# Reordering and pacing the dense work beside the first recurrence of a two-layer hybrid backbone

## Chip, cores and metric

One core of one Trainium2 chip runs the whole program. The metric is the device time of one execution in microseconds; the lower the better.

## What is computed

A backbone of two layers over a stream of 1024 latent tokens and 256 context tokens, width 1024. The context is a prefix that goes through the same weights and never reads the latents. Cut to what matters here:

```
for l in range(DEPTH):                        # DEPTH = 2
    last = l == DEPTH - 1
    ux = _modulate(h, norm1_g[l], sh1, sc1) @ w_in[l]          # latents
    uc = _modulate(hc, norm1_g[l], mc[0], mc[1]) @ (w_in[l])   # context
    # bidirectional RWKV-7: context scan from zero state, latent scan from the context's final state
    y_rwkv_x, y_rwkv_c = _rwkv_mixer(ux[..., :RWKV_COLS], uc[..., :RWKV_COLS], not last, ...)
    # four head groups of 256 channels: RWKV, pooling, Fourier, convolution; then one projection
    h = h + gt1 * _mix_and_project(ux, y_rwkv_x, *other)       # concat(...) @ w_out
    h = h + gt2 * _swiglu(_modulate(h, norm2_g[l], sh2, sc2), ffn_w_in[l], ffn_w_out[l])
    if not last:
        hc = hc + mc[2] * _mix_and_project(uc, y_rwkv_c, *other)
        hc = hc + mc[5] * _swiglu(_modulate(hc, norm2_g[l], mc[3], mc[4]), ffn_w_in[l], ffn_w_out[l])
return _rmsnorm(h, final_norm_g)
```

In the last layer the context is needed for the scan's starting state only: it has no output projection and no feed-forward there. `_swiglu` has a hidden width of 2816, that is 22 blocks of 128 ("features" below), each with a gate half and an up half.

## The kernel before

Channels lie on the 128 partitions, tokens along the free dimension. The latents are two blocks of 512 tokens (tb 0 and 1), the context one block of 256 (tb 2). A float32 product is made of three products of split operands: a high part (an ACT cast, line 318) and a low part (a subtraction on DVE or POOL, line 319), so that one block product over k channel blocks is 3k matmuls. All matmuls are issued from line 151, so the profile tells them apart by the PSUM tile: `ps`, `pb`, `pc` for the recurrence and the feed-forward, `pf` for the dense work beside the recurrence.

A layer runs in this order:

1. `rwkv1`: the first dense blocks, with the convolution beside them.
2. `rwkv2`: the recurrence, ten steps: two of the context (`it` 0 and 1), eight of the latents (`it` 2 to 9). Each step handles 128 tokens in each direction. Three iterations before step 0 only prepare. In a pass of the loop `chain` advances step `it`, `front_b` makes step `it + 1` ready, `inner` builds the triangular blocks of step `it + 2`, sends them through DRAM (lines 980 and 986, the tile `Ad`), solves them on DVE (lines 1026 to 1035) and sends the result through DRAM again (lines 1039 and 1045, `Td`), and `prep` makes the scaled inputs of step `it + 3` (up to line 956). `finish` reads out a block when both directions have passed it (the stores of line 1238). For the context this is at step 2, and sets `R.ctx`. A pass has 14 gaps (`GAPS`).
3. In each gap `W.fill(FILL[l][...])` lets a generator `fill()` issue dense work worth so many microseconds by its own count (256 columns x 6 matmuls count 0.64). The three numbers of `FILL[l]` hold for the first two passes, the third, and step 0 onwards. A yield of None ends a call without work. `fill()` goes through the rest of the input projection, the Fourier mixer (`four2`), the output projection of all groups but RWKV for the latents and of all groups for the context (`outp`), the context's second norm (`norm2c`) and its feed-forward for the first `NC` features (`ffn1_ctx`: four weight loads of 256 KB, split by ACT and POOL, 48 matmuls of 256 columns, a SiLU on line 1625). `side()` runs convolution and pooling and sets `R.sided` at its end.
4. Behind the recurrence: the RWKV part of the latents' output projection and their second norm (`ffn1_acts`), with what is left in `fill()` beside it.
5. `ffn1`: 22 features with the latents' products in a seven-product form, a copy `P1` on line 1564 each. For features from `NC` on, in layer 0, it also makes the context's products (48 matmuls of 256 columns) from weights that are split already, with one more split (`a21`).
6. The second half of the feed-forward and, in layer 0, the next layer's norm and first blocks.

Instructions are not issued in the program's order alone: a planner orders each engine's queue by the program's order and a simulated readiness, including whether a tile of a pool is free. The pool of general tiles, `t2`, has 73 (`T2`); the recurrence's rings (`rg`) take theirs once and give them back after their last use. Weight splits of `outp` use the pools `m2` and `f2`, those of `ffn1_ctx` `m2` and `c2`. All DMAs are issued from SP's queue in order. During the recurrence `lo_eng` is POOL.

Of the kernel before, what the change touches and what calls it, by code (L numbers as in the profile page):

```python
# [22 lines left out]
NFF = 22  # L23
# [18 lines left out]
MODPE = ((3, 0),)  # L42
MK = 7
FR = "c2"
FILL = ((2.6, 1.2, 0.9), (2.3, 1.0, 0.9))
LA = 2
NC = 14
ORD = (1, 0)
OFILL = (1.0, 0.3, 0.8, 1.0)
LOP = (0, 2, 4)  # L50
# [40 lines left out]
class _Kernel:  # L91
# [701 lines left out]
    def rwkv2(s, R, fill):  # L793
# [7 lines left out]
        for it in range(-3, N):  # L801
# [9 lines left out]
            for g in range(GAPS):  # L811
# [21 lines left out]
                W.step()  # L833
                W.fill(FILL[R.l][min(max(it + 2, 0), 2)])
            for _ in ch:
# [6 lines left out]
        while W.live:  # L842
            W.step()
            W.fill(FILL[R.l][2])

# [398 lines left out]
    def run(s, nlayers):  # L1244
# [43 lines left out]
        for l in range(nlayers):  # L1288
            last = l == L - 1
            segs = ("x",) if last else ("x", "c")  # L1290
            tbs = [tb for tb in range(3) if TBS[tb][0] in segs]
            swA, swB = [s.t2(), s.t2()], [s.t2(), s.t2()]
            ymix = [s.dr.tile([128, 1280], F32, name=s.nm("ymix")) for k in range(NK)]
            ho = [s.dr.tile([128, 1280], F32, name=s.nm("ho")) for k in range(NK)]
            hd = [s.dr.tile([128, 1280], F32, name=s.nm("hd")) for _ in range(NK)]
# [13 lines left out]
            R = _Rwkv()  # L1309
            R.conv1 = R.pool1 = R.rest2 = R.sided = R.ctx = False  # L1310

            def fill():
                for x in s.rest(l, R, acts, segs):
                    s.mod_step()
                    yield x
                assert not s.mods
                R.rest2 = True
                yield from s.four2(R, segs, swB, ymix)
                while not R.sided or not (last or R.ctx):
                    yield None  # L1320
                for tb in tbs[::-1]:
                    yield from s.outp(l, tb, hd, ho, ymix)
                if not last:
                    yield from norm2c()
                    for f in range(NC):
                        yield from s.ffn1_ctx(l, f, [a[2] for a in acts2], hid[f])

            def norm2c():

                for _ in range(2):  # L1330
                    yield
                s.lab("norm2")
                hc = s.rows(NK, ("c",))
                for k in range(NK):
                    h2[k][2] = hc[k][2]
                    nc.sync.dma_start(hc[k][2], ho[k][:, 1024:1280])
                yield
                r = yield from s.rstd_g([h2[k][2] for k in range(NK)], 256, D, 0, False, "ps", lambda j: s.t2())
                for k in range(NK):
                    acts2[k][2] = s.act_row(("c",))[2]  # L1340
                for _ in s.norm_g(l, 1, h2, 2, acts2, r):
                    if _ % 2:
                        yield
# [9 lines left out]
            s.weave.start(side())  # L1353
            s.rwkv1(l, R, first, acts, ("x", "c") if not last else ("x",), segs, swA, ymix, start)
            s.rwkv2(R, fill())
            h, acts = h2, acts2

# [131 lines left out]
    def ffn1_weights(s, l, ctx):  # L1489
# [11 lines left out]
        def sp(x):  # L1501
            hi, lo = s.t2(F32R, "f2"), s.t2(F32R, "f2")
            nc.scalar.copy(hi, x)  # L1503
            s.nw += 1
            (nc.gpsimd if s.nw % 7 in LOP else nc.vector).tensor_tensor(lo, x, hi.bitcast(F32), ALU.subtract)  # L1505
            return hi, lo
# [3 lines left out]
        for f in range(NFF):  # L1510
# [9 lines left out]
            yield sp(a12)  # L1520
            if ctx and f >= NC:
                yield sp(a21)
# [6 lines left out]
    def ffn1(s, l, wg, acts, B, bc, hid):  # L1529
# [4 lines left out]
        def take():  # L1534
            while len(q) <= LA:
                w = next(wg, None)
                if w is None:
                    break
                q.append(w)
            return q.pop(0)  # L1540
# [15 lines left out]
        for f in range(NFF):  # L1556
            s.lab("ffn")
            ctx = bc[0] is not None and f >= NC
            w = take()
# [316 lines left out]
```

## Time and profile before

| | |
|---|---|
| three runs, median (lowest to highest) | 3379.47 us (3378.45 to 3383.02) |
| profiled execution, its time | 3374.46 us |
| span from the first to the last instruction | 3372.7 us |
| mean granted TensorE clock | 0.907 |
| PE, DVE, ACT, POOL busy | 88%, 64%, 37%, 42% of the span |

Busy shares are means over stages that differ. `pf<-t,c` in a row means: the tile `pf` is written from tiles `t` and `c`, buffer numbers left out. A windows row gives the stretch in us from the span's start, its length, then for each engine the busy time in us and in brackets the number of instructions, then the granted clock, the busy share of the DMA engines and GB/s. PEld is the weight load, which overlaps PE. With a tile's name the row counts that tile's instructions alone, while clock and DMA stay those of the whole stretch. The stretches of the steps are cut at the first chain copy of each step (line 1139).

### The profile page before, as it was taken

To read this page: it belongs to the slowest core of one execution; us is meant where nothing else is said; L and a number is where in the kernel's file an instruction comes from. 1 tells how busy PE (TensorE), PEld (TensorE's weight loads), DVE (VectorE), ACT (ScalarE), POOL (GpSimd) and SP (SyncE) were. 2 spreads that over 40 slices of the span, in tenths; PEclk is the share of its full clock that TensorE was granted. 3 is DMA by queue.
4 is the path that set the end of the run, shared out by engine and by line. 5 is a ranking of instruction groups with operands and counts; after the bars stand their busy time and mean duration, and the time that the engine had idled before them with its cause. 6 is when DMAs were issued, how large, how long until landed. Compare 5 with 4: busy or idle time off the path is not lost.

```text
span 3372.7 us, 52579 instructions
## 1 busy us (share of the span) xinstructions
PE 2980.7 (88%) x18872; PEld 2405.8 (71%) x18872; DVE 2147.3 (64%) x3683; ACT 1260.6 (37%) x2575; POOL 1413.6 (42%) x1570
## 2 busy tenths in 40 slices
PE   6968897787998999999999978887877699999998
PEld 3757765665687788888888766655655478888887
DVE  6799756657556988644445598665666665555435
ACT  4455434443464222223212455343333433333312
POOL 2366324555258554435310064244542265444600
PEclk8979887787899999999999988977876899999999
DMA  7433335455464444337412212444553422223512
GB/s 263 152 99 103 100 114 139 132 154 156 135 228 131 145 137 153 118 98 232 142 35 77 87 53 94 119 139 124 162 151 76 139 76 75 91 79 124 179 39 77
DMA packets 375820, 415.50 MB, mean 123 GB/s; under 512 B 115587, under 2 KB 214916, under 8 KB 375558
## 3 DMA queue, kind: packets, MB, share of 16 engines
q1 hardware_dynamic: 375558, 412.13, 39.4%
q8 instruction: 149, 2.44, 0.3%
q14 instruction: 113, 0.93, 0.1%
HBM read 306.49 MB, written 100.27 MB: 121 GB/s over the span
## 4 chain that ended last, share of the span: by engine, by line
PE 58%; DVE 20%; DMA 12%; issue 4%; ACT 2%; POOL 2%; SPq 2%; DVEq 0%; POOLq 0%; ACTq 0%
PE pc L151 18%; PE ps L151 17%; PE pb L151 14%; PE pf L151 9%; DVE c L525 3%; DMA t<-Ad 3%; DMA Td<-t 2%; DVE t L1033 1%; DVE t L1026 1%; DVE t L941 1%; DMA t<-Td 1%; DVE t L255 1%; DMA t<-in_wmod 1%; DVE t L1035 1%; DVE g L1034 1%
## 5 line engine op out<-in xcount | busy, mean ns | idle before, releaser
L151 PE MATMUL pc<-t,f 128*128 128x512 f32 (+1 forms) x3108 | 750.2, 391 | 34.4 <-ACT t L420 21.4
L151 PEld LDWEIGHTS pc<-t,f 128*128 128x128 f32 x3108 | 580.2, 195 | 164.0 <-ACT t L420 25.3
L151 PE MATMUL ps<-t,f 128*128 128x512 f32 (+1 forms) x2094 | 519.9, 393 | 20.1 <-ACT t L318 7.9
L151 PE MATMUL pb<-t,f 128*128 128x512 f32 (+1 forms) x2094 | 468.5, 369 | 10.9 <-ACT t L1456 6.7
L151 PEld LDWEIGHTS ps<-t,f 128*128 128x128 f32 x2094 | 391.3, 190 | 101.5 <-ACT t L318 8.4
L151 PEld LDWEIGHTS pb<-t,f 128*128 128x128 f32 x2094 | 369.4, 189 | 81.4 <-ACT t L1456 7.4
L1503 ACT CAST f<-c 128x512 fp32r<-128x512 f32 x316 | 195.8, 621 | 531.0 <-PE ps L151 122.1
L1505 POOL TENSOR_TENSOR f<-c,f 128x512 fp32r<-128x512 f32 x135 | 184.3, 1365 | 428.2 <-ACT f L1503 404.3
L151 PE MATMUL pf<-t,f 128*128 128x512 f32 (+2 forms) x1500 | 311.2, 362 | 22.2 <-DMA f<-eo 8.3
L318 ACT CAST f<-m 128x512 fp32r<-128x512 f32 (+1 forms) x236 | 135.4, 576 | 437.3 <-PE pb L151 228.4
L151 PEld LDWEIGHTS pf<-t,f 128*128 128x128 f32 (+1 forms) x1500 | 247.6, 197 | 67.4 <-issue 9.7
L523 POOL TENSOR_TENSOR c<-c,cp 128x352 f32<-128x352 f32 (+2 forms) x168 | 186.3, 1109 | 152.1 <-ACT c L516 91.5
L1505 DVE TENSOR_TENSOR f<-c,f 128x512 fp32r<-128x512 f32 x181 | 159.9, 884 | 139.5 <-ACT f L1503 136.1
L151 PE MATMUL pf<-c,f 128*128 128x512 f32 (+1 forms) x704 | 214.8, 439 | 10.9 <-DVE t L1668 6.8
L319 POOL TENSOR_TENSOR t<-c,t 128x512 fp32r<-128x512 f32 (+1 forms) x110 | 138.4, 1298 | 161.2 <-PE ps L151 100.0
L151 PE MATMUL ps<-t,t 64*128 64x128 f32 (+2 forms) x1032 | 158.4, 341 | 43.4 <-DVE t L941 20.0
L525 DVE SCALAR_TENSOR_TENSOR c<-c,dv,c 128x352 f32<-128x352 f32 (+2 forms) x238 | 191.5, 838 | 1.0
L151 PEld LDWEIGHTS ps<-t,t 64*128 64x128 f32 (+1 forms) x1032 | 132.5, 230 | 70.0 <-issue 20.1
L151 PE MATMUL pc<-t,t 128*64 128x64 f32 (+3 forms) x2484 | 143.4, 250 | 40.3 <-ACT t L1161 20.7
L151 PEld LDWEIGHTS pc<-t,t 128*64 128x64 f32 (+2 forms) x2484 | 116.1, 154 | 84.2 <-issue 32.3
L151 PEld LDWEIGHTS pf<-c,f 128*128 128x128 f32 x704 | 140.0, 227 | 44.4 <-DVE t L1668 8.0
L255 DVE SCALAR_TENSOR_TENSOR cp<-m,sc,cp 128x512 f32<-128x512 f32 x140 | 137.3, 1001 | 45.9 <-DMA m<-in_wmod 45.2
(256 smaller groups left out, 4792.9 us busy)
## 6 DMA issues: line engine op xcount, KB each, us to landing
c<-in_ffin SPq DMA_DIRECT2D x176, 256.0 KB
m<-in_wmod SPq DMA_DIRECT2D x116, 256.0 KB
t<-rw SPq DMA_DIRECT2D x232, 128.0 KB
hid<-t SPq DMA_DIRECT2D x88, 256.0 KB
c<-hid SPq DMA_DIRECT2D x88, 256.0 KB
m<-in_ffout SPq DMA_DIRECT2D x80, 256.0 KB
t<-in_wmod SPq DMA_DIRECT2D x76, 256.0 KB
m<-in_win SPq DMA_DIRECT2D x64, 256.0 KB
```

The lines of the kernel that those rows point to most:

```text
L151: s.nc.tensor.matmul(o, l, r, start=start, stop=stop)
L255: nc.vector.scalar_tensor_tensor(acc[t], w, sc, acc[t], ALU.mult, ALU.add)
L318: s.nc.scalar.copy(hi, src)
L319: (eng or s.lo_eng).tensor_tensor(lo, src, hi.bitcast(F32), ALU.subtract)
L523: nc.gpsimd.tensor_tensor(g, g, t_, ALU.add)
L525: nc.vector.scalar_tensor_tensor(a, w[:, j:j + m], tap(j), a, ALU.mult, ALU.add)
L941: nc.vector.tensor_tensor(BKv[rows, :, :, 1 - h, :], cv(kd)[rows], cv(iP)[rows], ALU.mult)
L1026: nc.vector.tensor_tensor(tv, at(x, o, [0, m], [1, 4], [32, 4]), at(T_, r0, [32, m], [0, 4], [1, 4]), ALU.mult)
L1033: nc.vector.tensor_tensor(tv, at(x, o + 4, [0, m], [1, n], [32, 4]), at(T_, r0, [32, m], [0, n], [1, 4]), ALU.mult)
L1034: nc.vector.tensor_reduce(uv, tv, mybir.AxisListType.X, ALU.add)
L1503: nc.scalar.copy(hi, x)
L1505: (nc.gpsimd if s.nw % 7 in LOP else nc.vector).tensor_tensor(lo, x, hi.bitcast(F32), ALU.subtract)
```

## The change

In layer 0's `FILL` the calls of the third preparing pass are worth 1.5 in place of 1.2, those from step 0 on 1.6 in place of 0.9. `NC` is all 22 features in place of 14, so `ffn1` has no context products any more. In `fill()` the latents' two blocks of the output projection come first, with no wait for `R.ctx`; that wait follows, and then the context's block. Layer 1 issues the same work as before.

```
-FILL = ((2.6, 1.2, 0.9), (2.3, 1.0, 0.9))
+FILL = ((2.6, 1.5, 1.6), (2.3, 1.0, 0.9))
 LA = 2
-NC = 14
+NC = NFF
...
                 yield from s.four2(R, segs, swB, ymix)
-                while not R.sided or not (last or R.ctx):
+                while not R.sided:
                     yield None
-                for tb in tbs[::-1]:
+                for tb in (1, 0):
                     yield from s.outp(l, tb, hd, ho, ymix)
+                while not (last or R.ctx):
+                    yield None
                 if not last:
+                    yield from s.outp(l, 2, hd, ho, ymix)
                     yield from norm2c()
                     for f in range(NC):
                         yield from s.ffn1_ctx(l, f, [a[2] for a in acts2], hid[f])
```

## Rows read from the trace of the kernel before

**Rows 1.** Chain that ended last: start us, us, what; steps 3 to 6.

```profile
644.12 9.71 DMA m<-in_wout
...
743.58 9.90 DMA t<-Ad
...
782.68 7.63 DMA Td<-t
```

**Rows 2.** Windows, all engines: steps 2, 3, 5 and 8 of layer 0.

```profile
575.00:620.00 45.00, 29.16 (x341) 21.98 (x341) 31.54 (x81) 19.07 (x51) 18.18 (x40) 0.77 0.37 100
620.00:675.00 55.00, 44.87 (x425) 39.23 (x425) 38.94 (x87) 21.74 (x55) 33.12 (x51) 0.71 0.53 148
...
720.00:762.00 42.00, 33.78 (x340) 26.43 (x340) 22.70 (x58) 16.85 (x46) 21.58 (x41) 0.79 0.51 133
...
861.00:893.00 32.00, 32.00 (x331) 24.09 (x331) 13.36 (x32) 11.88 (x30) 10.00 (x12) 0.96 0.55 157
```

**Rows 3.** Windows of the tile pf alone (PE, PEld, DVE, ACT).

```profile
575.00:620.00 45.00, 0.38 (x1) 0.19 (x1) 0.00 (x0) 0.00 (x0) 0.77 0.37 100
620.00:675.00 55.00, 27.14 (x135) 23.14 (x136) 1.91 (x4) 0.00 (x0) 0.71 0.53 148
...
720.00:762.00 42.00, 15.21 (x46) 9.43 (x46) 2.24 (x3) 0.00 (x0) 0.79 0.51 133
...
810.60:940.00 129.40, 62.69 (x258) 44.02 (x259) 7.52 (x11) 0.77 (x2) 0.88 0.50 144
```

**Rows 4.** Windows, all engines: four longer stretches, the last of layer 1.

```profile
528.60:810.60 282.00, 210.84 (x2270) 170.85 (x2268) 183.25 (x444) 116.58 (x303) 154.27 (x268) 0.78 0.53 144
810.60:940.00 129.40, 112.41 (x1118) 86.77 (x1119) 71.66 (x158) 53.80 (x128) 46.63 (x53) 0.88 0.50 144
...
1117.00:1354.00 237.00, 237.00 (x1093) 197.84 (x1092) 198.76 (x261) 71.06 (x121) 119.63 (x83) 0.99 0.43 142
...
2539.00:2633.00 94.00, 64.95 (x773) 47.53 (x772) 52.30 (x139) 30.94 (x78) 13.24 (x24) 0.74 0.29 75
```

**Rows 5.** Single lines, 477 to 1100: ns min/median/max, first to last start, forms.

```profile
L1625 ACT ACTIVATE cp<-pf x14: 373/384/385, 935.6 to 1084.2; 128x256 f32<-128x256 f32 x14
...
L1668 DVE SCALAR_TENSOR_TENSOR t<-pf,mod,t x24: 467/742/752, 640.7 to 902.8; 128x512 f32<-128x512 f32 x16, 128x256 f32<-128x256 f32 x8
...
L1336 SPq DMA_DIRECT2D t<-ho x8: 319/425/473, 815.0 to 835.4; - x8
...
L1238 SPq DMA_DIRECT2D ymix<-t x20: 371/428/1457, 611.1 to 939.7; - x20
...
L956 POOL TENSOR_TENSOR t<-t,pcs x8: 608/659/882, 766.4 to 816.1; 128x256 f32<-128x256 f32 x8
```

**Rows 6.** Single lines: layer 1's readout stores, then P1 copies in stretches.

```profile
L1238 SPq DMA_DIRECT2D ymix<-t x16: 319/423/1619, 2572.4 to 2632.5; - x16
...
L1564 ACT COPY t<-ps x7: 582/582/583, 2737.1 to 3079.8; 128x512 f32<-128x512 f32 x7
...
L1564 ACT COPY t<-pc x5: 578/582/584, 1117.1 to 1353.4; 128x512 f32<-128x512 f32 x5
...
L1564 ACT COPY t<-pb x3: 586/586/586, 1379.0 to 1530.8; 128x512 f32<-128x512 f32 x3
```

**Rows 7.** Groups of instructions, 1049 to 1085, behind the recurrence.

```profile
L151 PE MATMUL pf<-t,c 128*128 128x256 f32 x243 | 30.1, 283 | 0.0
...
L319 POOL TENSOR_TENSOR c<-m,c 128x512 fp32r<-128x512 f32 x17 | 22.4, 1342 | 8.1 <-ACT c L318 6.5 <-PE pf L151 1.3
```

**Rows 8.** Two solves: product line 1026, and windows of all engines.

```profile
L1026 DVE TENSOR_TENSOR t<-t,t x8: 180/452/1209, 652.0 to 677.7; 128x16 f32<-128x16 f32 x1, 128x32 f32<-128x32 f32 x1, 128x48 f32<-128x48 f32 x1, 128x64 f32<-128x64 f32 x1
...
652.00:679.00 27.00, 18.36 (x237) 16.16 (x236) 25.81 (x59) 13.06 (x32) 20.60 (x31) 0.81 0.56 164
...
L1026 DVE TENSOR_TENSOR t<-t,t x8: 172/332/657, 2569.6 to 2592.0; 128x16 f32<-128x16 f32 x1, 128x32 f32<-128x32 f32 x1, 128x48 f32<-128x48 f32 x1, 128x64 f32<-128x64 f32 x1
...
2569.00:2593.00 24.00, 20.26 (x334) 15.56 (x329) 19.21 (x57) 12.02 (x32) 6.75 (x14) 0.83 0.46 118
```

## What the change should do to the time

> **What bounds the kernel now.** I read the page first, then the chain of waits, then windows over the steps of layer 0's first recurrence, first of all engines and then of the dense tile pf alone, and last the answers for single lines that date the parts. Layer 1 has the same recurrence without a context to finish, and serves as a measured version of "no dense work left over". The page's busy share of PE hides three stages.
>
> In layer 0's recurrence (steps 1 to 9 and a tail, 528.6 to 940) the first six steps are bound by a round trip, not by PE. In a step the block of A is sent round by DMA (743.6 to 753.5, 9.9 us), the triangular solve runs on DVE until its result leaves (782.7, 29 us later), and the way back takes another 7.6 us [rows 1]. A step lasts as long with dense work as without: 45 us with one dense matmul on pf (575 to 620), 42 us with 15 us of them (720 to 762) [rows 2, 3]. Over steps 1 to 6 PE is busy 210.8 of 282 us at a granted clock of 0.78: 71 us idle [rows 4]. Step 8 has no later step to prepare and is the opposite: PE busy 32.0 of 32 us [rows 2].
>
> Behind the recurrence lies a stretch that still holds dense work. The 14 context features that were meant to lie beside the recurrence have their SiLU between 935.6 and 1084.2, so all 14 end behind the last chain step [rows 5]. From the last readout store (939.7) to the third P1 copy of the feed-forward (1117.1) layer 0 takes 177 us; layer 1, with no such features, 105 us (2632.5 to 2737.1) [rows 5, 6].
>
> In the feed-forward PE is busy 237.0 of 237 us [rows 4]. A feature without context takes 236.3/12 = 19.69 us (the pc copies come every third feature, five of them); one with context (1530.8 - 1379.0)/6 = 25.30 us [rows 6].
>
> **The change part by part.** *Eight context features leave the feed-forward:* 8 x (25.30 - 19.69) = **-45 us** there. They come back as ffn1_ctx features with the same 48 matmuls of 256 columns, but their weights are loaded and split anew: 4 loads of 256 KB, 4 ACT casts and 4 POOL differences of 1.34 us a feature, less the split of a21. PE's price of such a feature is 30.1 x 48/243 = 5.95 us [rows 7]. The splits cost nothing of their own as long as POOL's 4 x 1.34 = 5.4 us lie beside that; POOL is busy 47 and ACT 54 of 129 us in steps 7 to tail [rows 4]. Without that cover a feature would cost POOL's time on top.
>
> *The order.* The latents' projection needs no context readout. Before, the context's first readout store is at 611.1, the first projection result at 640.7, the last at 902.8 [rows 5]. I count the calls of fill: 14 a step, worth 0.9 us each before and 1.6 after. The Fourier mixer owes 31 us, a latent block 0.6 + 30.7 us and 4 empty calls, the context block 0.8 + 20.5 us and 4 empty calls, its norm about 10 calls, a feature 5.12 us. Before, that gives the context in steps 2 to 4, the latents in 4 to 10 and every feature behind, as the rows show. After, it gives the latents in steps 1 to 4.1, the context to 5.4, its norm to 6.1, and then features, some 20 of 22 by the end of the tail. No wait is added: the wait for the context's readout now comes at step 4, when that readout (step 2) is past. The queue that the block is moved past is SP's: 36 more issues fall into steps 1 to 6, and a step's A transfers stand behind them. One such case is on the chain, 9.7 us of a w_out load at 644 [rows 1].
>
> *What goes into steps 1 to 6.* Some 9 latent output blocks that run after 810.6 now run before it (11 DVE results on pf there, two of them features) [rows 3]. 9 x 18 = 162 matmuls of 512 columns at 62.7/258 = 0.24 us are 39 us, against 71 us idle. What the stretch of the steps can be: nothing, or less than nothing, if length stays independent of dense work. At the upper end PE, which takes its queue in order, puts a chunk that is 0.7 us longer (0.9 us at clock 0.78) before each of some 15 dependent groups a step: 13.5 us a step, 81 us. The nearest row is the step with the context's projection, 55 us long with 27 us on pf, ten more than the step without [rows 2, 3]. With 39 us going into 71 idle I take 4 us a step, nearer to the lower end: **+24 us**.
>
> The clock could take that away. The step without dense work has 29.2 - 0.4 = 28.8 us of PE's own matmuls at clock 0.77; the step at 720 has 33.8 - 15.2 = 18.6 us, ten less [rows 2, 3]. The Trainium skill (TensorE: Matmul & The Clock Gate, Part 1) says that the slow clock is the default and that activity releases it; the trace agrees in the ten microseconds, though the mean clocks (0.77 and 0.79) hardly differ. By that rule the steps would not stretch, and the sum would be 24 us lower; this is the first rival.
>
> *Steps 7 to the tail.* The features cannot start at their turn. Rings and small weights hold 69 of the 73 t2 tiles (counted in the code), and the context's norm wants 4 for the rows and 8 for the activations. They come free with the last prep: its last difference is at 816.1, and the loads of the eight context rows are issued from 815.0 [rows 5]. So steps 7 to tail become a stretch bound by PE. They take 129.4 us with 112.4 us of PE, 62.7 of it on pf; the other 49.7 us stay [rows 3, 4]. In come 20.5 x 5.95 = 122 us, and 5 us for the norm and the start of the pipe: 177 us, **+47 us**. Bounds: +35 at the feed-forward's 5.6 us a feature with no loss, +60 if PE idles a tenth.
>
> *The stretch behind* falls from 177 us to layer 1's 105 and some 4 us for the features left over, which lie beside the norm: **-69 us** (-60 to -73).
>
> *POOL against DVE.* A solve with POOL busy 20.6 of 27 us takes 25.7 us from its first to its last product line, one with POOL busy 6.8 of 24 us 22.4 us [rows 8]: 3.3 us for 48 points of POOL's share. The 18 more splits of the latent blocks are at most 18 x 1.34 = 24 us in 282 [rows 7], 8.5 points, 0.6 us a step, and lie inside the 4 us. The Trainium skill (SBUF — State Buffer, "SBUF: two separate sides") says that a DVE instruction with two SBUF inputs and a GpSimd instruction lock each other out for their whole length; it speaks against this change. By it those 24 us could be paid once more, and the sum would be -19 us; the trace agrees in direction, with 3.3 us in place of the 14 us that POOL was busier.
>
> **The sum:** 24 + 47 - 69 - 45 = -43 us. On the profiled execution's 3374.5 us that is 3331.5; the median of the runs lies 5.0 us above that execution, so **3336 us**.
>
> **The rivals.** *More* (22%): the idle 71 us and the better clock take the latent blocks without stretch, and a feature costs 5.6 us: 0 + 38 - 69 - 45 = -76 us, 3303. For it: length has not followed dense work. Against: the 55 us step.
>
> *The chunks delay the chain* (15%, slower): the longer pieces before each dependent group, in steps 1 to 6, at 13.5 us a step: 81 + 47 - 69 - 45 = +14 us, 3393. It decides once the mean step grows from 47 past 58 us (24 + 43 = 67 us over six steps). For it: PE's order, and that steps 7 to tail last 129 us here and 94 in layer 1, which has no dense work in them [rows 4]. Against: the step at 720 is shorter than the empty one.
>
> *The features still run behind* (13%; the change does not do what it says): the tiles come free later, or the planner lets the chain go first. Then steps 7 to tail shrink to layer 1's 94 us (-35), and 8 x 5.95 = 48 us more go into the stretch behind: 24 - 35 + 48 - 45 = -8 us, 3371.
>
> My forecast has 45%; 5% are for none of these.
>
> **How the numbers follow.** The runs spread by 0.1%, so 0.2% (6.8 us) is about what can be told from no change. Faster: nearly all of the 45 and 22, half of the 13, little of the rest: 0.74. Same: 0.10, the other half of the third rival and the edge of the second. Slower: 0.16. The forecast's own range is 3310 to 3362 (stretch 0 to 40, tail +35 to +60, behind -73 to -60). For 8 in 10 it reaches beyond "more" to 3290, and past the third rival to the second's 3393: 3290 to 3394.
>
> **What would show it.** First latent projection result by 570, all projection results by about 740; the context rows loaded when the last prep ends; 22 SiLUs, most between 830 and 1010; last readout store near 1010; 105 to 115 us from there to the third P1 copy; every feature of the feed-forward at 19.7 us. Wrong if steps 1 to 6 average over 58 us, if the features run behind the last readout, or if features without context slow down.

## The result, and the profile after

The changed kernel takes 3418.18 us (median of four runs, 3412.74 to 3419.63) beside 3381.24 us for the kernel before: a ratio of 1.0117 [1.0089, 1.0145], so 1.2% slower, where 43 us less were forecast. The profiled execution spans 3410.9 us, 38 us more than before.

The trace, cut where the prediction cut it:

| stretch | before, us | after, us | difference | forecast |
|---|---|---|---|---|
| start to step 0 | 477.6 | 478.8 | +1.2 | 0 |
| step 0 | 51.0 | 56.1 | +5.1 | 0 |
| steps 1 to 6 | 282.0 | 330.7 | **+48.7** | +24 |
| steps 7 to tail | 129.1 | 183.8 | +54.6 | +47 |
| stretch behind: last readout store to third P1 copy | 177.4 | 143.9 | **-33.5** | -69 |
| feed-forward: third to last P1 copy | 413.7 | 369.5 | -44.2 | -45 |
| the rest | 1841.8 | 1847.9 | +6.1 | 0 |
| sum | 3372.7 | 3410.9 | +38 | -43 |

The feed-forward came out as forecast and the tail nearly so. Two terms are far off: the steps (30 us with step 0) and the stretch behind (35 us).

Windows of all engines after: step 1, steps 2, 7 and 8, steps 0 to 6, steps 7 to the tail, the stretch behind, and the feed-forward's counterpart of the third row of [rows 4].

```profile
534.90:606.60 71.70, 54.72 (x461) 41.65 (x460) 35.83 (x92) 20.95 (x56) 40.17 (x63) 0.79 0.56 162
606.60:657.50 50.90, 39.89 (x382) 31.03 (x382) 36.64 (x75) 25.53 (x63) 31.87 (x46) 0.81 0.59 175
...
865.70:947.90 82.20, 67.95 (x661) 60.64 (x659) 40.47 (x93) 33.13 (x72) 43.03 (x44) 0.91 0.52 143
947.90:987.70 39.80, 39.80 (x489) 35.81 (x489) 12.50 (x22) 23.93 (x50) 23.89 (x21) 0.97 0.64 191
...
478.80:865.60 386.80, 309.85 (x2981) 242.72 (x2980) 231.72 (x532) 159.43 (x407) 212.34 (x342) 0.80 0.53 151
865.60:1049.40 183.80, 169.26 (x1724) 153.64 (x1722) 76.11 (x153) 91.62 (x186) 105.98 (x95) 0.95 0.55 163
...
1049.40:1193.40 144.00, 102.13 (x485) 76.67 (x486) 129.07 (x165) 55.07 (x95) 60.42 (x37) 0.79 0.50 167
1193.40:1429.00 235.60, 235.60 (x1057) 195.62 (x1057) 161.46 (x210) 72.64 (x123) 117.95 (x85) 1.00 0.35 118
```

Windows after of the tile pf alone: steps 0 to 6, steps 1 to 6, then step 7, step 8, the rest of the tail in two parts, the stretch behind.

```profile
478.80:865.60 386.80, 167.18 (x667) 117.70 (x666) 20.04 (x34) 3.59 (x9) 0.80 0.53 151
...
534.90:865.60 330.70, 144.37 (x614) 108.28 (x614) 17.47 (x30) 0.77 (x2) 0.82 0.53 150
...
865.70:947.90 82.20, 50.14 (x337) 45.24 (x335) 2.93 (x7) 2.69 (x7) 0.91 0.52 143
947.90:987.70 39.80, 28.23 (x201) 25.08 (x201) 1.70 (x4) 1.53 (x4) 0.97 0.64 191
987.70:1020.00 32.30, 24.70 (x183) 22.46 (x184) 1.67 (x4) 1.52 (x4) 1.00 0.53 168
1020.00:1049.40 29.40, 26.70 (x210) 25.27 (x208) 1.69 (x4) 1.77 (x5) 1.00 0.56 172
1049.40:1193.40 144.00, 10.97 (x62) 10.91 (x62) 0.88 (x4) 0.13 (x1) 0.79 0.50 167
```

Three things are to be seen. First, in steps 0 to 6 PE idles 386.8 - 309.9 = 77 us; before it idled 333.0 - 253.3 = 80 us. The dense work that came in (pf 167 us for 104) did not go into the idle time: the steps grew by 54 us, PE's work by 57. Secondly, steps 7 to the tail hold 931 matmuls on pf (337 + 201 + 183 + 210) in 129.8 us, 0.139 us each. Thirdly, the stretch behind holds only 11 us of pf, so the features did move out of it, and yet it is 39 us longer than layer 1's 105 us; its fullest engine is DVE, with 129 of 144 us.

Single lines after: the SiLUs, the projection's results, the loads of the context rows, the readout stores, the preps' last difference.

```profile
L1628 ACT ACTIVATE cp<-pf x22: 377/384/386, 851.3 to 1049.2; 128x256 f32<-128x256 f32 x22
...
L1671 DVE SCALAR_TENSOR_TENSOR t<-pf,mod,t x24: 465/739/752, 564.9 to 779.3; 128x512 f32<-128x512 f32 x16, 128x256 f32<-128x256 f32 x8
...
L1339 SPq DMA_DIRECT2D t<-ho x8: 346/422/2461, 753.0 to 790.0; - x8
...
L1238 SPq DMA_DIRECT2D ymix<-t x20: 365/424/1479, 644.9 to 1049.4; - x20
...
L956 POOL TENSOR_TENSOR t<-t,pcs x32: 605/612/862, 487.3 to 869.4; 128x256 f32<-128x256 f32 x32
```

The order came true: first projection result at 564.9 (640.7 before, [rows 5]), last one at 779.3 (902.8), all 22 SiLUs by the last readout store (1049.4, against 939.7). But the steps themselves ran later: the last difference of a prep starts at 869.4 instead of 816.1.

### The profile page after: what moved, and what is told of

It reads as the page before. It is cut to its first block, busy times and chain, and to the rows that moved or that the text cites. A ratio compares the mean times of both kernels' runs of the same rounds, so it can differ in the third digit from the quotient of the medians.

```text
span 3410.9 us, 52667 instructions
## 1 busy us (share of the span) xinstructions
PE 3005.4 (88%) x18872; PEld 2421.8 (71%) x18872; DVE 2147.9 (63%) x3678; ACT 1285.6 (38%) x2606; POOL 1446.3 (42%) x1599
## 4 chain that ended last, share of the span: by engine, by line
PE 55%; DVE 21%; DMA 13%; issue 4%; ACT 3%; SPq 2%; POOL 2%; DVEq 0%; POOLq 0%; ACTq 0%
PE pc L151 16%; PE ps L151 16%; PE pb L151 14%; PE pf L151 8%; DVE c L525 4%; DMA t<-Ad 3%; DMA Td<-t 2%; DVE t L1033 2%; DVE t L1026 1%; DVE t L941 1%; DMA t<-in_wmod 1%; DMA Ad<-t 1%; DMA t<-Td 1%; DVE t L1035 1%; DVE t L255 1%
## 5 line engine op out<-in xcount | busy, mean ns | idle before, releaser
L151 PE MATMUL pc<-t,f 128*128 128x512 f32 (+1 forms) x3108 | 755.6, 393 | 43.7 <-ACT t L420 20.5
L1506 ACT CAST f<-c 128x512 fp32r<-128x512 f32 x308 | 191.2, 621 | 561.6 <-PE ps L151 151.2
L1508 POOL TENSOR_TENSOR f<-c,f 128x512 fp32r<-128x512 f32 x132 | 175.5, 1329 | 484.4 <-ACT f L1506 461.3
L151 PE MATMUL pf<-t,f 128*128 128x512 f32 (+2 forms) x1116 | 261.3, 389 | 22.8 <-DMA f<-eo 10.3
L151 PEld LDWEIGHTS pf<-t,f 128*128 128x128 f32 (+1 forms) x1116 | 198.1, 199 | 66.7 <-issue 10.4
L1508 DVE TENSOR_TENSOR f<-c,f 128x512 fp32r<-128x512 f32 x176 | 150.2, 856 | 116.2 <-ACT f L1506 116.1
```

The source lines that it names most:

```text
L151: s.nc.tensor.matmul(o, l, r, start=start, stop=stop)
```

## Experiments

Each is an edit of the changed kernel, of the kernel before or of `order_only`, with the kernel before beside it on the same chip; the ratio is to that kernel. The lengths are those of its own trace in us; "behind" is the stretch behind.

| run | order | features | call's worth from step 0 | steps 0-6 | 7-tail | behind | ratio |
|---|---|---|---|---|---|---|---|
| before | old | 14 | 0.9 | 333.0 | 129.1 | 177.4 | 1 |
| after | new | 22 | 1.6 | 386.8 | 183.8 | 143.9 | 1.0117 [1.0089, 1.0145] |
| mods_held | new | 22 | 1.6 | 384.3 | 182.9 | **117.2** | 1.0046 [1.0027, 1.0065] |
| pace_back | new | 22 | 0.9 | **338.1** | **124.9** | 200.2 | 0.997 [0.9953, 0.9988] |
| nc_back | new | 14 | 1.6 | 387.2 | 158.7 | 139.6 | 1.0165 [1.0136, 1.0193] |
| order_only | new | 14 | 0.9 | 335.7 | 125.3 | 150.5 | **0.9946** [0.9929, 0.9964] |
| order_held | new | 14 | 0.9 | 335.3 | 125.8 | 151.2 | 0.9938 [0.9915, 0.996] |
| pace_mid | new | 14 | 1.2 | 354.2 | 142.0 | 135.5 | 1.0012 [0.9996, 1.0029] |
| pace_only | old | 14 | 1.6 | 360.7 | 148.5 | 146.8 | 1.0061 [1.0046, 1.0076] |
| late_pace | new | 14 | 0.9, 1.6 from step 7 | 332.8 | 155.1 | 140.3 | 0.9988 [0.9975, 1.0001] |
| order_slower | new | 14 | 0.7 | 330.4 | 105.1 | 194.4 | 0.9968 [0.9953, 0.9983] |
| order_chain_first | new | 14 | 0.9 | 340.8 | 111.0 | 192.8 | 0.9954 [0.9938, 0.9971] |
| chain_first | new | 22 | 1.6 | 363.5 | 240.4 | 144.8 | 1.012 [1.0092, 1.0148] |

Third to last P1 copy is 369 to 376 us with 22 features outside the feed-forward, 407 to 417 with 14, in every trace.

**The stretch behind: what took the features' place on DVE.** Groups of instructions on DVE after, 1049.4 to 1193.4:

```profile
L255 DVE SCALAR_TENSOR_TENSOR cp<-m,sc,cp 128x512 f32<-128x512 f32 x59 | 56.5, 999 | 3.6 <-DMA m<-in_wmod 3.5
L1460 DVE TENSOR_TENSOR t<-t,t 128x512 fp32r<-128x512 f32 x12 | 14.4, 1212 | 0.0
```

Line 255 sums the next layer's modulation, from weights loaded into `m2`, into `cp`. Before, the whole 177 us behind the recurrence hold 14 of these sums (18.5 us), the first at 1085.6. Now 59 stand there, 56.5 us of DVE, between the second norm's own instructions (line 1460). In `mods_held` the sums read their factor from a copy that waits for the norm's last tile:

```
+        s.sc2 = s.cpool.tile([128, 8, 2], F32, name=f"sc2_{l}")
+        nc.vector.scalar_tensor_tensor(s.sc2.rearrange("p a b -> p (a b)"), X[7][0][:, 0:16], 0.0,
+                                       s.sc.rearrange("p a b -> p (a b)"), ALU.mult, ALU.add)
...
-                sc = s.sc[:, k, t:t + 1]
+                sc = (s.sc2 if s.sc2 is not None else s.sc)[:, k, t:t + 1]
```

> The changed kernel, with the modulation sums that run beside the feed-forward made to wait for the latents' second norm (their factor is a copy that reads the last tile of that norm, times zero, plus the old factor; the values stay the same). Theory A: behind the recurrence the planner pulls these sums into the 144 us up to the third P1 copy (56.5 us of DVE on line 255 there), in front of the norm's DVE work; held back, the stretch falls to 105 to 115 us and the whole to about 3385 us (3378 to 3392), less what the sums cost later. Rival: the stretch is long because layer 0 takes the norm of the first latent block before the second block's projection, as it has no dense work left; then it stays at 135 us or more and the whole at 3410 or above.

Windows of all engines of `mods_held`, the stretch behind, and its DVE group of the same line:

```profile
1047.50:1164.70 117.20, 85.94 (x431) 63.64 (x432) 91.85 (x112) 54.48 (x94) 55.98 (x37) 0.85 0.44 154
```

```profile
L256 DVE SCALAR_TENSOR_TENSOR cp<-m,sc,cp 128x512 f32<-128x512 f32 x14 | 16.5, 1213 | 0.0
```

With 14 sums in place of 59 the stretch takes 117.2 us: 26.7 us of the 39 above layer 1's length were the sums. The other 12 stayed. The feed-forward, which takes the sums back, is 6 us longer (375.8 for 369.5). Layer 1 has no next layer, so the twin that I took lacks this work.

The sums follow the features. In every kernel whose calls are worth 0.9 or less the stretch behind holds 14 of them; with a higher worth, and nothing to hold them, it holds more: 28 in `late_pace`, 31 in `pace_mid`, 56 to 59 in `pace_only`, `nc_back` and the change. The first one starts shortly after the last SiLU of the context's features: 0.7 us later in `order_only` (1063.0 and 1063.7), 1.4 in the kernel before, 9.3 in the changed one. That the buffers `m2` and `cp` hold the sums until then is read from the program and not tested.

**The pace.** `pace_back` is the changed kernel with the old worth of a call.

```
-FILL = ((2.6, 1.5, 1.6), (2.3, 1.0, 0.9))
+FILL = ((2.6, 1.2, 0.9), (2.3, 1.0, 0.9))
```

> The changed kernel with the calls of fill at their old worth (1.2 and 0.9); the new order and all 22 features stay. Theory P: the larger pieces in front of the chain's matmuls made steps 0 to 6 longer (387 us against 333); with the old worth they return to within 10 us of 333, all features run behind the last step, the stretch there grows to about 225 us and the whole is about 3385 us (3375 to 3395). Rival Q: the early loads of the output weights on SP's queue do it; then steps 0 to 6 stay above 360 us and the whole is about 3415 us.

Windows of `pace_back`, steps 0 to 6 and steps 7 to the tail, and its SiLUs:

```profile
478.00:816.10 338.10, 260.32 (x2668) 191.01 (x2668) 217.96 (x508) 136.93 (x367) 180.30 (x314) 0.81 0.53 149
816.10:941.00 124.90, 106.95 (x1231) 91.71 (x1231) 75.59 (x166) 60.96 (x136) 56.52 (x58) 0.92 0.51 152
```

```profile
L1628 ACT ACTIVATE cp<-pf x22: 362/380/384, 909.0 to 1108.5; 128x256 f32<-128x256 f32 x22
```

The steps lose 49 us and the tail 59; the stretch behind takes 56 back, as most features now run there. The new order, with its early issues on SP's queue, stayed, and the steps shrank all the same: at the old pace these issues don't stretch them. What stretched them is the pace, with the loads and splits that come with it (below). Two more runs put the single parts against it.

```
nc_back, from the changed kernel:      -NC = NFF    +NC = 14
order_only, from the kernel before:    -while not R.sided or not (last or R.ctx):   +while not R.sided:
                                       and the context's block behind the wait, as in the change
```

> The changed kernel with 14 features beside the recurrence and 8 in the feed-forward, as before; the new order and the new worth of the calls stay. Theory P: steps 0 to 6 stay at about 387 us; steps 7 to the tail lose 8 features of 5.95 us and fall from 184 to about 136 us; the feed-forward takes its 45 us back; the whole stays within 10 us of the changed kernel's 3418. Theory B (the backlog of features that the planner puts in front of the chain in step 7 costs more than its own matmuls): steps 7 to the tail fall by clearly more than 48 us and the whole is under 3405 us.

> The kernel before with the new order of the output projection alone (latents first, no wait for the context's readout), old worth of the calls, 14 features. Theory P: steps 0 to 6 as before within 10 us (333), the features still all behind the last step, the whole 3375 to 3390 us. Rival Q (early loads on SP's queue): steps 0 to 6 above 360 us and the whole at 3405 us or more.

`nc_back` left steps 0 to 6 as they were and took 25 us off the tail, 48 were due, while the feed-forward got its features back: no faster than the change itself (1.0165 beside 1.0117, intervals that overlap a little). Its tail holds 26 of the modulation's sums, and PE idles 30 us of it where it idled 14.5 in the change; how much of the missing 23 us that makes is not shown. `order_only` is the fastest so far, where I had expected no gain. Taken in this order, the ratios of the change come apart as -0.5% for the order, +0.2% for the eight features (0.9946 to 0.997, intervals that overlap) and +1.5% for the pace (0.997 to 1.0117); 0.7 of the 1.5 are the sums that `mods_held` holds back. The parts do not simply add: with 14 features the pace costs 2.2% under the new order (0.9946 to 1.0165) and 0.6% under the old (`pace_only`, below), so the order that gains 0.5% at the old pace loses 1.0% at the new. A feature behind the recurrence costs (663.2 - 611.5)/8 = 6.5 us by the sums of the three stretches of `pace_back` and `order_only`, one in the feed-forward 5.4.

**How the steps grow with the pace.** `pace_mid` sets 1.2 in `order_only`; `pace_only` is the kernel before with the new `FILL` alone.

> New order, 14 features, calls worth 1.2 in the third preparing pass and 1.2 from step 0 on. Steps 0 to 6 were 336 us at 0.9 and 387 us at 1.6 with the new order. If the stretch grows evenly with the worth, 358 us and the whole about 3375 us, above the order alone (3354); if it sets in only where pieces outgrow what the weights' supply allows, 336 to 345 us, and the whole at 3345 to 3358 us.

> The kernel before with the new worth of the calls alone (1.5 and 1.6; old order, 14 features). Theory P: with the old order dense work is missing in steps 1 and 2 (it waits for the context's readout), so that these stay at about 46 us, and the steps after them stretch as with the new order (50 to 59 us, step 7 to 60 or more); steps 0 to 6 at 345 to 365 us, the whole slower than before by 10 to 30 us. Rival: the stretch needs the new order; steps 0 to 6 stay within 8 us of 333 and the whole is at or below before.

Windows of `order_only`, steps 0 to 6, all engines and then pf alone:

```profile
477.70:813.40 335.70, 261.21 (x2668) 191.97 (x2668) 216.38 (x506) 136.90 (x368) 180.44 (x314) 0.80 0.54 150
```

```profile
477.70:813.40 335.70, 131.24 (x392) 77.72 (x392) 15.29 (x24) 2.80 (x7) 0.80 0.54 150
```

The same of `pace_mid`:

```profile
478.00:832.20 354.20, 280.26 (x2884) 211.38 (x2884) 221.26 (x530) 146.70 (x384) 195.41 (x326) 0.85 0.56 157
```

```profile
478.00:832.20 354.20, 147.54 (x536) 95.81 (x536) 19.11 (x32) 2.81 (x7) 0.85 0.56 157
```

From before to `order_only` pf grows by 27 us (104.05 to 131.24) and the steps by 2.7: PE's other matmuls fall from 149.2 to 130.0 us, at a granted clock of 0.77 and 0.80, and pay for most of it. From there on nothing is free: to `pace_mid` pf grows by 16.3 us and the steps by 18.5; to the change pf by 35.9 and the steps by 51.1. PE's idle time in steps 0 to 6 is 80, 74.5, 74 and 77 us in these four kernels, and 77 in `pace_only`. So from 0.9 to 1.6 the dense work lies on top of the steps' waits. That idle time is no fixed sum, though: in `order_slower`, at 0.7 a call and a granted clock of 0.73, PE's other matmuls take 163 us and it idles 58.5, in steps as long as at 0.9.

```profile
477.00:807.40 330.40, 271.84 (x2568) 202.78 (x2570) 221.44 (x514) 128.25 (x345) 171.32 (x307) 0.73 0.51 142
```

**What the dense work brings with it.** Is it the wait for fresh weights, the load and split work, or the matmuls? In the first kernel below layer 0's projection in the recurrence and the context's features multiply by one resident pair of split weights, while the loads and splits still run; the second, whose edit is shown, has neither.

```
-            w = s.wload(s.I["wout"][l, cb], ks[0] * 128)
+            w = s.fixed(l)[ks[0]:] if l == 0 else s.wload(s.I["wout"][l, cb], ks[0] * 128)
...
-            w = s.wload(s.I["ffin"][l, i * NFF + f], tag="c2", eng=nc.gpsimd)
+            w = s.fixed(l)
```

> The changed kernel, but layer 0's output projection in the recurrence and the context's features multiply by one resident pair of split weights (so these products are not the reference's). Every weight is still loaded by DMA and split by ACT and POOL; only PE does not wait for it. Theory W (at the larger worth PE's queue puts dense matmuls in front of the chain whose weights are not there yet, and the chain stands behind them): steps 0 to 6 fall from 387 us to 350 or less and step 7 from 82 to 60 or less. Rival L (the dense matmuls' own PE time stretches the steps): both stay within 10 us.

> The same without the loads and splits of these weights (left out; the products are not the reference's). Theory W: steps 0 to 6 and step 7 as in the run whose weights are not waited for, within 10 us. Rival C (the load and split work itself, on DMA, ACT and POOL, delays the solves and preps): clearly shorter than that run, by 15 us or more over steps 0 to 7. Rival L: both stay near 387 and 82 us.

One run each: 3411.99 and 3353.41 us beside 3376.43. Steps 0 to 6 take 405.3 us without the wait and 367.6 without the work. So taking away the wait of the matmuls for their weights does not shorten these steps; it does shorten step 7, from 82.2 to 65.7 us, and without the work that is 48.2. The work that makes them is worth 38 us between these two, and 19 against the change itself, whose steps hold fewer dense matmuls (667 on pf; about 790 and 780 in these two). Even without it some 30 us remain above `order_only` and `pace_back`. Two more runs have the loads alone and the splits (of a resident tile) alone:

> As the run with resident weights (layer 0's output projection in the recurrence and the context's features multiply by one resident pair; the products are not the reference's), but every weight is loaded by DMA and then not split. With loads and splits, steps 0 to 6 were 405 us and steps 7 to tail 168; with neither, 368 and 146. Theory D (SP's queue and the DMA engines: the loads delay the A transfers and the solve's results): 390 us or more, and 160 or more. Rival S (the splits on ACT and POOL delay the preps and the solves): within 10 us of 368 and 146.

> The same with the splits and without the loads: each time a resident raw tile is split by ACT and POOL anew, nothing is loaded (the products are not the reference's). Theory D: within 10 us of 368 and 146. Rival S: 390 us or more over steps 0 to 6, and 160 or more from 7 to the tail. If both halves lie between, they share it.

Windows of steps 0 to 6, of the kernel without the wait, with neither, with the loads, with the splits:

```profile
478.60:883.90 405.30, 328.20 (x3137) 260.03 (x3135) 247.00 (x554) 165.40 (x420) 226.73 (x355) 0.83 0.53 151
```

```profile
479.60:847.20 367.60, 305.58 (x3090) 245.22 (x3090) 217.59 (x553) 131.25 (x353) 151.03 (x289) 0.82 0.46 132
```

```profile
480.30:883.90 403.60, 318.13 (x3093) 251.68 (x3092) 216.88 (x555) 131.38 (x352) 150.29 (x289) 0.80 0.69 203
```

```profile
480.80:877.80 397.00, 316.91 (x3092) 251.57 (x3090) 247.97 (x539) 172.54 (x431) 236.24 (x365) 0.82 0.42 117
```

Loads alone add 36 us (3385.08 us in all), splits alone 29 (3388.99), both 38. They do not add up: each is nearly the whole price. A good part of what they add is idle time of PE, 62 us with neither, 85.5 with the loads, 80 with the splits, 77 with both: unlike the matmuls, they do lengthen the waits. The loads alone wait for no split and run ahead, with the DMA engines busy 0.69 of the time, more than in any other kernel here; so I take its 36 us as an upper end for the loads of the change, which stands at 0.53.

**Where the pace would be worth it, and the planner.** `late_pace` keeps 0.9 up to step 6 and sets 1.6 from step 7 on; `order_held` is `order_only` with the sums held back; `order_slower` sets 0.7.

```
-                W.fill(FILL[R.l][min(max(it + 2, 0), 2)])
+                W.fill(FILL[R.l][3 if it >= 7 else min(max(it + 2, 0), 2)])
```

> The new order, 14 features and the old worth (1.2 and 0.9) up to step 6; 1.6 only from step 7 on, where no prep is left. Theory: in steps 7 to 9 the features and the chain share a PE that is nearly full, so what the steps gain in features they lose in length: steps 7 to tail grow from 125 by as much as the stretch behind falls from 150, and the whole is within 8 us of the order alone (3354). Rival: the stretch behind shrinks by more, since the sums of the modulation and the norm run freely, and the whole falls by 10 us or more; or the weights' loads delay the last solves and step 7 again exceeds 60 us.

> The new order alone (old worth, 14 features) with the modulation sums made to wait for the latents' second norm. Theory A': in the order alone the 14 features still hold the buffers of these sums for most of the 150 us behind the last step, so that few are pulled in; the whole is within 8 us of the order alone (3354). Rival: they cost there too what they cost with no features left, and the whole falls by 15 us or more.

> The order alone with calls worth 0.7 in place of 0.9 from step 0 on (14 features). If the steps are at their floor at 0.9 (the round trip of the solve), steps 0 to 6 stay at 330 to 340 us, more dense work lands behind the recurrence, and the whole is 5 to 20 us above the order alone (3354). If pieces still cost at 0.9, steps 0 to 6 fall below 325 us and the whole does not rise.

`late_pace` adds 30 us to the tail and takes only 10 from the stretch behind, where I had expected an even exchange; 28 sums stand there in place of 14, and that pace with the sums held back was not run. At 0.7 the steps lose 5 us against 0.9, so they are near their floor; the tail loses 20 and the stretch behind gains 44. With 14 features at 0.9 holding the sums changes nothing: the features are there up to 1063.0, and only 14 sums follow with or without the hold.

The last two give the recurrence's instructions the planner's priority over the dense work.

```
-                if g % 2 == 0:
-                    W.next(ch, None)
-                W.step()
+                with s.ahead(SPRI):
+                    if g % 2 == 0:
+                        W.next(ch, None)
+                    W.step()
```

> The changed kernel with every instruction of the recurrence's own parts (chain, preparation, solve, readout; convolution and pooling too while they last) given a higher priority with the planner than the dense work. Theory O (the planner's order: dense pieces, and the backlog of features in step 7, stand in front of the chain on PE's queue): steps 0 to 6 fall from 387 us to under 360, step 7 from 82 to under 60, the whole under 3395 us. Rival R (the amount of work in a step, on PE, DMA, ACT and POOL, whatever its order): steps 0 to 6 stay above 375 us and the whole above 3405 us.

> The order alone (old worth, 14 features) with the same higher priority. Theory O: little is left to gain at the old worth, steps 0 to 6 at 320 to 340 us (336 without), the whole within 10 us of 3354. Rival: also at the old worth pieces stand in front of the chain, and steps 0 to 6 fall below 320 us.

`chain_first` starts the recurrence 11 us earlier and has steps 0 to 6 23 us shorter than the change, but a tail of 240 us: the A blocks of the last two solves are read back 124 us apart, at 751.3 and 875.6. In those steps PE is as busy as in the change and idles 54 us for 77, but 140 of the recurrence's own matmuls have left them (2739 - 565 on pf, for 2981 - 667).

```profile
467.90:831.40 363.50, 309.76 (x2739) 224.19 (x2740) 198.00 (x492) 135.07 (x352) 177.99 (x293) 0.81 0.52 147
```

What the priority gives, it loses behind; at 0.9 it changes the time as little (0.9954 for 0.9946). It doesn't tell whether the 30 us left are the planner's order or the sheer amount of matmuls; that stays open.

## Why the prediction was wrong, step by step

**"With 39 us going into 71 idle I take 4 us a step": failed, and it is the larger miss in cost.** The size of the work was off, 58.6 us more on pf in steps 1 to 6 (85.75 to 144.37) where I counted 39. My 0.24 us a matmul was the mean of two shapes: of the 258 in that row 107 have 256 columns, and the 512-column ones took 0.32 us each, so my 162 come to some 50 us. Besides, at 1.6 a call 133 matmuls of the context's features fall into these steps, 26 us. Groups on PE, before (810.6 to 940), then after (534.9 to 865.6):

```profile
L151 PE MATMUL pf<-c,f 128*128 128x512 f32 x133 | 42.5, 439 | 0.0
```

```profile
L151 PE MATMUL pf<-t,c 128*128 128x256 f32 x133 | 26.1, 352 | 6.4 <-DVE t L383 3.4 <-DVE cp L1629 2.4 <-ACT t L382 0.6
```

And the idle time took none of it: PE idled 71 us of steps 1 to 6 before and 70 after. That a step is as long with dense work as without [rows 2, 3] was read from steps at 0.9 a call, and there it holds (`order_only`: +27 us on pf, +2.7 us); it does not go on to 1.2 or 1.6. Between 19 and 38 of the 54 us come with the loads and splits of the dense work (`weights_resident`, against the change and against its twin that waits for none); the splits I had put at 0.6 us a step; the loads I had named, as issues in front of the A transfers, and given no price. The rest stays without loads and splits, so it goes with the matmuls; its mechanism is open.

The Trainium skill (SBUF — State Buffer, "SBUF: two separate sides") has a DVE instruction with two SBUF inputs and a GpSimd instruction that reads SBUF lock each other out. The runs agree in direction: splits alone add 85 us of POOL and 29 us to the steps, and DVE is busy 30 us longer with 14 instructions fewer (539 for 553). It cannot be the only route, as the loads alone add 36 us with both unchanged.

**"The stretch behind falls to layer 1's 105": failed.** It fell by 33.5 us, not 69. Layer 1 has no next layer's modulation; with the features gone early from `m2` and `cp`, 45 more of these sums ran on DVE, ahead of the norm that the feed-forward waits for. `mods_held` shows 26.7 of the 35 us.

**"Steps 7 to the tail +47": right in kind, 8 us short.** They are bound by PE (169.3 of 183.8 us). What is left beside pf is 54.0 us, as forecast (49.7 + 5), but by luck: PE's other work fell to 39.5 us, and it idled 14.5. On pf it is 129.8 us in place of 122: 931/48 = 19.4 features at 48 x 0.139 = 6.7 us, where I had 20.5 at 5.95. In step 7, 82 us long, the chain's copies of its own result are done by 883.2. Single line, then PE in order of time (start us, us, what, in brackets the idle time before it):

```profile
L1152 ACT COPY t<-pc x2: 367/368/368, 882.5 to 882.8; 64x256 f32<-64x256 f32 x2
```

```profile
882.35 1.69 PE L151 MATMUL pf<-t,c 128*128 128x256 f32 x12
...
884.35 2.90 PE L151 MATMUL pf<-t,c 128*128 128x256 f32 x22
...
890.36 7.40 PE L151 MATMUL pf<-t,c 128*128 128x256 f32 x58 [0.84 <-POOL c L319]
...
904.31 0.51 PE L151 MATMUL pf<-t,c 128*128 128x256 f32 x2 [3.41 <-DVE t L1035]
905.72 3.68 PE L151 MATMUL pf<-t,c 128*128 128x256 f32 x16 [0.90 <-POOL c L319]
909.23 0.60 PE L151 MATMUL pc<-gg,cv 128*128 128x256 f32 x2
```

The chain's next matmuls follow at 909.2, 26 us later: dense matmuls stand before them, and PE idles 5 us there, 1.7 of it for the splits of POOL. My rival had such delays at 0.9 us for each dependent group in steps 1 to 6; here one costs a large part of a step, in step 7, which takes 43.8 us in `pace_back`.

**"The tiles come free with the last prep": failed as a date.** The context rows are loaded at 753.0 to 790.0, while preps run until 870. It moved no sum by itself.

**"Eight features leave the feed-forward: -45": right,** -44.2, and a feature without context takes 19.42 us ((1542.9 - 1193.4)/18, between the first and last copy from pc). Of the order's dates the first came true (first result before 570); the last result came 40 us later than I said.

**The slower rival** named the right sign with another balance. Its limit, a mean step above 58 us, was not reached (55.1); the time was lost at 55 us because the stretch behind gave back half of what I had set against it. On the clock, the other rival: at 0.80 for 0.77 PE's own matmuls did shrink (149.2 to 142.7 us in steps 0 to 6), but the steps stretched anyway, so a better clock did not pay for the work. The ten microseconds from which I read it were not the clock's alone: the step at 720 has 294 matmuls beside pf, the empty one 340.

**What beats both kernels:** the order alone, 0.9946 [0.9929, 0.9964] (3354.00 us beside 3369.59). At 0.9 a call the projection without the wait starts the 14 features 29 us earlier (first SiLU 906.3 for 935.6), and the stretch behind falls from 177.4 to 150.5 us.

## What to carry to other kernels

That a stage has taken dense work free of charge at one pace says nothing of a higher one: check, by the idle time that remains, whether the added work went into the waits or on top of them, and price its loads and splits as well as its matmuls. A stretch of another layer is a measure only if it has the same work waiting for the buffers that come free. And change the order of work and its pace in separate runs and together: here the order gave 0.5% at the old pace and took 1.0% at the new.

## What I had not expected of the hardware

PE's idle time in steps 0 to 6 hardly moved over five kernels, 74 to 80 us, while its busy time went from 253 to 310 us; it did move where the worth of a call fell to 0.7 (58.5 us) and where the loads and splits went (62 us) or the recurrence had priority (54 us). And taking away both the loads and the splits frees 38 us, but either one of them alone brings back 29 to 36.
